# One layer of a hybrid diffusion block: attention scores of both maps on the two halves of the array, exponentials in SBUF, tanh for the gate, one reciprocal root for all heads

## The chip, the cores and the metric

The kernel runs on one core of a Trainium2 chip. The metric is the device time of one execution in microseconds (us); the median of several runs counts.

## What is computed

One mixer layer works on 512 latent tokens and 256 context tokens, 1024 channels wide. One input projection feeds three branches: A, a gated linear recurrence in both directions (LRU); B, differential attention with 8 heads; C, a gated MLP over chunks of 128 positions (SGU). Each is multiplied by a gate path and projected; the three are merged by sigmoid gates, projected once more and normalized. The change touches branch B most:

```python
def diff_attn_core(q, k, v, lam):
    s = jnp.einsum('bqhmd,bkhmd->bhmqk', q.astype(f32), k.astype(f32)) * (DIFF_HEAD_DIM ** -0.5)
    p = jax.nn.softmax(s, axis=-1)
    w = p[:, :, 0] - lam * p[:, :, 1]
    return jnp.einsum('bhqk,bkhe->bqhe', w, v.astype(f32)).astype(v.dtype)

def diff_head_out(o, g, lam_init):
    of = o.astype(f32)
    of = of * lax.rsqrt(jnp.mean(jnp.square(of), axis=-1, keepdims=True) + RMS_EPS)
    of = of * g.astype(f32) * (1.0 - lam_init)

def merge_branches(h_a, g_a, attn, g_b, sgu, g_c, gates, w_branch, w_out):
    y_a = (h_a * jax.nn.silu(g_a)) @ w_branch[0]
    y_b = (attn * jax.nn.silu(g_b)) @ w_branch[1]
    y_c = (sgu * jax.nn.silu(g_c)) @ w_branch[2]
    s_a, s_b, s_c = jnp.split(jax.nn.sigmoid(gates), N_BRANCH, axis=-1)
    return (s_a * y_a + s_b * y_b + s_c * y_c) @ w_out
```

Here m counts the two maps of a head (64 channels each), so a head has 128 channels of q and k.

## The kernel before

All matrix products keep single precision by splitting each operand into a high and a low part (`split`, L53 to L55: ACT casts the high part, DVE subtracts for the low one) and adding three products, high x high, high x low and low x high (`mm3`, L57 to L64). Weights stream from DRAM through three raw buffers on the SP queue (L100, L103); ACT casts the high part (L121), and POOL, or DVE from the LRU stage on, subtracts the low part (L122). Tile pools decide when a buffer comes free. PE runs its matmuls in the order of the program; the other engines are ordered by a list scheduler, with priorities and with the small pieces of work (`chore`, `drain`) placed by their stated costs.

The stages follow each other:
- *Head*: modulation, the projections q, k and kc of heads 0 and 1, and v.
- *Attention loop*, 32 steps (8 heads, 4 blocks of 128 queries). A table (`fill`, L158 to L171) puts the projections of later heads between the steps. A step has the scores of both maps (`scores`, L695 to L708), the softmax (L710 to L723: DVE's maximum `mxn`, ACT's exponential `e` with its sum), the combination of the maps on DVE (L726 to L730), and, a step later, six transposes on PE (L735) and the split of the transposed weights (L746, L748). After a head's fourth block come the product with v (`values`), the mean square `ms` by a matmul with a matrix of ones (L761), Ln and Exp on ACT for the reciprocal root (L762, L763), and a product on POOL (L764). The gate of branch B is a Sigmoid on ACT (L670). These functions lie in different table sets of ACT, so ACT loads a table when it changes between them.
- *LRU stage*, 8 blocks of channels, software pipelined: block i + 1 is projected (`xa`, `xac`, then ACT's copies `pad`, L865 and L867), block i's gates `ri` are computed and pass through sigmoid, tanh and square (`decay`), `merge_gate(i - 1)` and `merge_b(i - 1)` multiply the gate `gt` and the projection `y` of branch B, which reads its operand from `hsB` (the split of `ob`, made ahead of the loop). The results `ha` go to DRAM (`pa_d`, L947) and come back later as `pa` (L1026).
- *SGU and the end*: `sv` (its PSUM tiles freed by `vz`, L1041, which adds a bias row `bvv`), gating, the projections of the other two branches, the output projection and the layer norm.

In the scores before, a head's q of map m stands with its high and low parts on the two halves of the partitions, and k likewise, so that one matmul over 128 rows adds two products:

```python
PE.matmul(sp[:, sl], qds[h][:, 2 * m + j, qs], kds[h][:, m, sl],
          start=(j == 0), stop=(j == 1))
```

For this layout `q_evac` (L527) and `k_split` (L554) work on 64 partitions at a time, and a DMA from POOL's queue copies each half of q to the other half. The exponentials of the second map are written over its scores in PSUM.

Of the kernel before, what the change touches and what calls it, by code (L numbers as in the profile page):

```python
# [10 lines left out]
F32 = mybir.dt.float32  # L11
# [18 lines left out]
def block_kernel(ctx, tc, x, c, cctx_in, c_ctx, w_ada, b_ada, w_in, b_in, conv_w, conv_b,  # L30
# [160 lines left out]
    for i in range(9):  # L191
        if i < 7:
            want("cm", win, (i + 1) * P)
        if i > 1:
            want("cm", win, D + (i - 2) * P)
        if i > 0:
            want("cm", win, 10 * D + (i - 1) * P)
            want("cm", w_branch[0, 1], (i - 1) * P)
# [25 lines left out]
    V.memset(tiny, 2.0 ** -100)  # L224
    sc16 = cp.tile([P, 16], F32, name="sc16")
# [18 lines left out]
    with tc.tile_pool(name="hd", bufs=1) as hd:  # L244
# [186 lines left out]
        S.preload_act_table_set("natural_log_exp_and_others")  # L431
# [4 lines left out]
        V.tensor_scalar(vbias, colC[:, 32:40], lam1, None, op0=ALU.mult)  # L436
        V.tensor_scalar(gcol, colB[:, 104:105], 1.0 - (0.8 - 0.6), None, op0=ALU.mult)
# [30 lines left out]
    at = tc.alloc_tile_pool(name="at", bufs=1, reuse_waits="tile")  # L468
    ropc = at.tile([P, T], F32, name="ropc")
# [3 lines left out]
    vhl, qds, kds, sbs = {}, {}, {}, {}  # L473
# [54 lines left out]
    def q_evac(h, ps):  # L528
        n = f"q{h}"
        z = z_evac(ps, bcol(16 + h), n)  # L530
        rope(z, n)


        def hi():
            qds[h] = at.tile([P, 4, T], F32R, tag="qd", bufs=2, name="qd" + n)
            qd = qds[h]
            for m in range(2):
                a = slice(64 * m, 64 * m + 64)
                if h < 2:
# [10 lines left out]
        chore(0.7, n, hi, 4 * h - 5)  # L550
        chore(0.6, n, lambda: fin(0))
        chore(0.6, n, lambda: fin(1))

    def k_split(n, h, z, sl):  # L554

        def hi():
            if h not in kds:
                kds[h] = at.tile([P, 2, TA], F32R, tag="kd", bufs=2, name=f"kd{h}")
            kd = kds[h]
            for m in range(2):  # L560
                a = slice(64 * m, 64 * m + 64)
                if n[1:] in "01":
                    S.copy(kd[a, m, sl], z[a])
                else:
                    V.tensor_copy(kd[a, m, sl], z[a])  # L565

        def lo(m):
            kd = kds[h]
            a, b = slice(64 * m, 64 * m + 64), slice(64 - 64 * m, 128 - 64 * m)
            V.tensor_tensor(kd[b, m, sl], z[a], f(kd[a, m, sl]), ALU.subtract)  # L570
        w = (sl.stop - sl.start) / 960
        chore(w + 0.15, n, hi, 4 * h - 5)
        chore(w + 0.07, n, lambda: lo(0))
        chore(w + 0.07, n, lambda: lo(1))
# [47 lines left out]
    def units(kind, i):  # L622
# [39 lines left out]
        def u():  # L662
# [7 lines left out]
            S.activation(sg, ps, AF.Sigmoid, bias=bcol(40 + i))  # L670
# [4 lines left out]
            S.preload_act_table_set("natural_log_exp_and_others")  # L675
# [14 lines left out]
    es, sms, wts = {}, {}, {}  # L690
# [4 lines left out]
    def scores(i):  # L695
# [4 lines left out]
        sps = []  # L700
        for m in range(2):
            sp = big_t(f"s{i}_{m}")
            for sl in (slice(0, 512), slice(512, TA)):
                for j in range(2):
                    PE.matmul(sp[:, sl], qds[h][:, 2 * m + j, qs], kds[h][:, m, sl],  # L705
                              start=(j == 0), stop=(j == 1))
            sps.append(sp)
        return sps  # L708

    def softmax(i, sps):  # L710
# [27 lines left out]
    def wt_split(i, tp):  # L738
        h, qt = divmod(i, 4)
        if qt == 0:  # L740
# [6 lines left out]
        with hp(0):  # L747
            V.tensor_tensor(wts[h][1][:, :, qs], src, f(wts[h][0][:, :, qs]), ALU.subtract)  # L748

    def values(h, alloc=acc_t):  # L750
# [3 lines left out]
        sq = at.tile([P, T], F32, tag="sq", bufs=1, name=f"sq{h}")  # L754
# [4 lines left out]
    def rms(h, sq):  # L759
        pm = (acc_t if h < 7 else big_t)(f"ms{h}")[:, 0:T]  # L760
# [65 lines left out]
    dr = ctx.enter_context(tc.tile_pool(name="dr", bufs=1, space=bass.MemoryType.DRAM))
# [452 lines left out]
```

## Time and profile before

| | us |
|---|---|
| median of 3 runs | 1040.11 (1037.9 to 1040.95) |
| the profiled execution | 1038.81 |
| its span | 1037.0 |
| PE busy | 974.0 (94%) |
| DVE busy | 663.6 (64%) |
| ACT busy | 526.1 (51%) |
| POOL busy | 155.7 (15%) |
| chain that ended last: PE, DVE, ACT, DMA | 66%, 16%, 10%, 4% |

A busy share is an average over the whole span. Waits are read place by place: a row of the waits gives the engine and line that waited, what released it, the time in all, how often, and the longest. PE's busy time counts matmuls with modelled ends, so neighbouring matmuls overlap in the records; the pace is read from their starts. The granted clock (PEclk) is a share of TensorE's full clock.

### The profile page before, as it was taken

How to read it: one execution, taken by the hardware profiler on the slowest of the kernel's cores; microseconds unless marked ns; L12 is line 12 of the kernel's file. 1: busy time of each engine (PE TensorE's matmuls, PEld its weight loads, DVE VectorE, ACT ScalarE, POOL GpSimd, SP SyncE). 2: the span in 40 equal slices, each digit the busy share in tenths (PEclk: the TensorE clock that was granted, in tenths of full speed). 3: DMA queues.
4: the chain of work that ended last, by engine and by line, in shares of the span. 5: the costliest groups of instructions: out<-in, count | busy, mean ns of one | idle time of the engine just before them, and what ended most of it. 6: DMA issues, size and time to landing. Idle time of an engine off the chain costs nothing.

```text
span 1037.0 us, 14225 instructions
## 1 busy us (share of the span) xinstructions
PE 974.0 (94%) x5719; PEld 844.0 (81%) x5719; DVE 663.6 (64%) x1024; ACT 526.1 (51%) x741; POOL 155.7 (15%) x117
## 2 busy tenths in 40 slices
PE   5997799989989998999999999599999999999996
PEld 4796688878878886888888888598889988888896
DVE  4479788788788663787777776348433356424567
ACT  3145856647647796897777794213231234332221
POOL 2143424333243252000000000000000000000002
PEclk8999999989989999999999999799999999999998
DMA  9933220130130132113333223534332232654312
GB/s 299 296 103 84 62 61 21 42 101 21 41 102 21 41 102 70 43 51 102 102 102 92 82 92 92 189 107 132 95 99 82 82 102 82 236 171 145 98 61 82
DMA packets 148184, 103.41 MB, mean 100 GB/s; under 512 B 3629, under 2 KB 143382, under 8 KB 148118
## 3 DMA queue, kind: packets, MB, share of 16 engines
q1 hardware_dynamic: 146054, 96.11, 30.4%
q0 software_dynamic: 1920, 6.29, 2.3%
q8 instruction: 45, 0.74, 0.3%
q14 instruction: 21, 0.17, 0.1%
q10 hardware_dynamic: 144, 0.10, 0.0%
HBM read 94.10 MB, written 4.19 MB: 95 GB/s over the span
## 4 chain that ended last, share of the span: by engine, by line
PE 66%; DVE 16%; ACT 10%; DMA 4%; issue 3%; SPq 1%; POOL 0%; POOLq 0%; ACTq 0%; DVEq 0%
PE y L62 4%; PE gt L62 4%; PE gt L64 4%; PE gt L63 4%; PE y L64 4%; PE y L63 4%; DVE mxn L715 2%; DVE e L730 2%; DVE kd L565 2%; PE out L62 1%; PE u L62 1%; PE u L64 1%; PE u L63 1%; PE out L64 1%; PE out L63 1%
## 5 line engine op out<-in xcount | busy, mean ns | idle before, releaser
L121 ACT CAST w<-raw 128x1024 fp32r<-128x1024 f32 x96 | 99.7, 1044 | 83.5 <-PE y L64 20.0
L122 DVE TENSOR_TENSOR w<-raw,w 128x1024 fp32r<-128x1024 f32 x71 | 86.4, 1222 | 66.9 <-ACT w L121 66.9
L62 PE MATMUL gt<-xhl,w 128*128 128x512 f32 x192 | 75.6, 394 | 1.3 <-ACT pad L865 1.3
L63 PE MATMUL gt<-xhl,w 128*128 128x512 f32 x192 | 74.8, 390 | 0.0
L64 PE MATMUL gt<-xhl,w 128*128 128x512 f32 x192 | 74.8, 390 | 0.0
L705 PE MATMUL s<-kd,qdq 128*128 128x512 f32 (+1 forms) x256 | 58.7, 368 | 15.6 <-ACT e L720 6.0
L122 POOL TENSOR_TENSOR w<-raw,w 128x1024 fp32r<-128x1024 f32 x25 | 61.0, 2445 | 67.4 <-ACT w L121 67.4
L705 PEld LDWEIGHTS s<-kd,qdq 128*128 128x128 f32 x256 | 44.5, 196 | 27.1 <-issue 12.7
L715 DVE TENSOR_REDUCE mxn<-s 128x1 f32<-128x768 f32 x64 | 58.3, 949 | 7.5 <-PE s L705 7.5
L720 ACT ACTIVATE e<-s,mxn 128x768 f32<-128x768 f32 x32 | 28.8, 900 | 50.9 <-DVE mxn L715 50.8
L1162 POOL PARTITION_BROADCAST grb<-grs x8 | 3.8, 581 | 322.4 <-DVE grs L1159 322.4
L62 PEld LDWEIGHTS gt<-xhl,w 128*128 128x128 f32 x192 | 36.1, 188 | 9.1 <-ACT pad L865 1.5
L64 PEld LDWEIGHTS gt<-xhl,w 128*128 128x128 f32 x192 | 36.0, 188 | 7.7
L63 PEld LDWEIGHTS gt<-xhl,w 128*128 128x128 f32 x192 | 36.1, 188 | 7.0
L947 POOL DMA_DIRECT2D pa_d<-ha x8 | 4.4, 551 | 227.4 <-DVE ha L946 227.4
L730 DVE SCALAR_TENSOR_TENSOR e<-s,sm,e 128x768 f32<-128x768 f32 x32 | 32.6, 1017 | 6.5 <-ACT e L723 5.7
L54 ACT CAST vh<-v 128x128 fp32r<-128x128 f32 x48 | 12.4, 264 | 42.7 <-PE v L64 19.5
L842 ACT ACT_TABLE_LOAD x25 | 32.1, 1283 | 0.5
L62 PE MATMUL xa<-xhl,w 128*128 128x512 f32 x64 | 26.3, 411 | 4.8 <-ACT pad L865 4.8
L748 DVE TENSOR_TENSOR wtl<-t,wth 128x768 fp32r<-128x768 f32 x32 | 30.3, 950 | 0.6 <-ACT wth L746 0.5
L723 ACT ACTIVATE e<-e,sm 128x768 f32<-128x768 f32 x32 | 29.9, 934 | 0.2 <-DVE sm L722 0.2
L842 ACT ACTIVATE rt<-ri,colB 128x770 f32<-128x770 f32 x32 | 27.7, 906 | 2.5 <-PE ri L64 1.8
(457 smaller groups left out, 3233.0 us busy)
## 6 DMA issues: line engine op xcount, KB each, us to landing
raw<-in_w_in_dram SPq DMA_DIRECT2D x96, 512.0 KB, 3.9
raw<-in_w_branch_dram SPq DMA_DIRECT2D x24, 512.0 KB, 4.0
ada<-in_w_ada_dram SPq DMA_DIRECT2D x6, 1024.0 KB, 9.6
qdq<-qdq POOLq DMA_DIRECT2D x16, 256.0 KB, 3.2
adg<-in_w_ada_dram SPq DMA_DIRECT2D x8, 512.0 KB, 6.6
raw<-in_w_out_dram SPq DMA_DIRECT2D x8, 512.0 KB, 3.4
xtok<-in_x_dram SPq DMA_DIRECT2D x4, 512.0 KB, 5.7
ada<-in_w_ada_dram SPq DMA_DIRECT2D x4, 512.0 KB, 5.9
```

What stands on the lines that cost most here:

```text
L62: PE.matmul(ps, ah, bh, start=(first and i == 0), stop=False)
L63: PE.matmul(ps, ah, bl, start=False, stop=False)
L64: PE.matmul(ps, al, bh, start=False, stop=(last and i == n - 1))
L121: S.copy(h, raws[j])
L122: state["lo"].tensor_tensor(l, raws[j], f(h), ALU.subtract)
L705: PE.matmul(sp[:, sl], qds[h][:, 2 * m + j, qs], kds[h][:, m, sl], start=(j == 0), stop=(j == 1))
L715: V.tensor_reduce(mxn[:, m:m + 1], sps[m][:, 0:TA], mybir.AxisListType.X, ALU.max, negate=True)
L720: S.activation(e, sps[m][:, 0:TA], AF.Exp, bias=mxn[:, m:m + 1], accum_out=sm[:, m:m + 1])
L723: S.mul(es[i][0], es[i][0], sm[:, 0:1])
L730: V.scalar_tensor_tensor(e0, e1, sm[:, 1:2], e0, op0=ALU.mult, op1=ALU.add)
L748: V.tensor_tensor(wts[h][1][:, :, qs], src, f(wts[h][0][:, :, qs]), ALU.subtract)
L842: order[0] = S.activation(out, in_, fn, **kw)
```

## The change

It does the following.
- q and k are kept in their natural layout: high and low parts each over 128 partitions, map 0 on the lower 64, map 1 on the upper 64. The splits take one instruction where they took two, and q's DMAs are dropped. The scores are twelve matmuls over 64 rows, the maps alternating between the two halves of the array (`tile_position`); the product of the low parts is left out, as everywhere else in the kernel.
- Both maps' exponentials go to SBUF.
- The gate's sigmoid is computed as 0.5 tanh(x/2) + 0.5, on ACT by Tanh and Identity.
- The mean square of each head comes from a matmul with 32 columns of ones on one quarter of the array's columns, and is copied into `msb`. Behind the last head one Ln and one Exp take all heads; the result goes through DRAM (`rs_d`) and comes back over all partitions, and DVE multiplies it into `ob` (`hs_b`). This and the split of `ob` stand behind step 0 (heads 0 to 3) and step 1 (heads 4 to 7) of the LRU loop.
- `merge_gate(i)` moves a step ahead, and its weight with it; `xa1` and `xac1` use the larger PSUM tiles; `macc` is allocated in step 1; `xac0` stands ahead of the last head's product.
- The bias row `bvv` is loaded ahead of `pa`, and the last block of `pa` is loaded from POOL's queue.
- Some tiles are allocated ahead of the stage that first uses them.

```diff
+    halfc = cp.tile([P, 1], F32, name="halfc")
+    hb = cp.tile([P, 8], F32, name="hb")
...
-        S.preload_act_table_set("natural_log_exp_and_others")
...
+    wts[0] = tuple(at.tile([P, 6, T], F32R, tag="wt" + n, name=f"wt{n}0") for n in "hl")
...
+    sqs0 = at.tile([P, T], F32, tag="sq", bufs=1, name="sq0")
+    msb = at.tile([P, 2, T], F32, name="msb")
...
-            qds[h] = at.tile([P, 4, T], F32R, tag="qd", bufs=2, name="qd" + n)
+            qds[h] = at.tile([P, 2, T], F32R, tag="qd", bufs=2, name="qd" + n)
...
+                V.tensor_scalar(qds[h][:, 0, :], z, 0.125, None, op0=ALU.mult)
...
+        def lo():
             qd = qds[h]
-            for m in range(2):
...
-            V.scalar_tensor_tensor(qd[a, 2 * m + 1, :], z[a], 0.125, f(qd[a, 2 * m, :]),
+            V.scalar_tensor_tensor(qd[:, 1, :], z, 0.125, f(qd[:, 0, :]),
                                    op0=ALU.mult, op1=ALU.subtract)
-            G.dma_start(qd[b, 2 * m:2 * m + 2, :], qd[a, 2 * m:2 * m + 2, :])
...
+                V.tensor_copy(kds[h][:, 0, sl], z)
...
+        def lo():
             kd = kds[h]
-            for m in range(2):
...
-            V.tensor_tensor(kd[b, m, sl], z[a], f(kd[a, m, sl]), ALU.subtract)
+            V.tensor_tensor(kd[:, 1, sl], z, f(kd[:, 0, sl]), ALU.subtract)
...
-            S.activation(sg, ps, AF.Sigmoid, bias=bcol(40 + i))
+            S.activation(sg, ps, AF.Tanh, bias=hb[:, i:i + 1], scale=0.5)
+            S.activation(sg, sg, AF.Identity, bias=halfc, scale=0.5)
...
-            S.preload_act_table_set("natural_log_exp_and_others")
...
-        for m in range(2):
-            sp = big_t(f"s{i}_{m}")
-            for sl in (slice(0, 512), slice(512, TA)):
-                for j in range(2):
-                    PE.matmul(sp[:, sl], qds[h][:, 2 * m + j, qs], kds[h][:, m, sl],
-                              start=(j == 0), stop=(j == 1))
+        sps = [big_t(f"s{i}_{m}") for m in range(2)]
+        for sl in (slice(0, 512), slice(512, TA)):
+            for j, (jq, jk) in enumerate(((0, 0), (0, 1), (1, 0))):
+                for m in range(2):
+                    a = slice(64 * m, 64 * m + 64)
+                    PE.matmul(sps[m][:, sl], qds[h][a, jq, qs], kds[h][a, jk, sl],
+                              start=(j == 0), stop=(j == 2), tile_position=(64 * m, 0))
...
-            e = sps[1][:, 0:TA]
-            if m == 0:
-                e = at.tile([P, TA], F32, tag="e0", bufs=2, name=f"e0_{i}")
+            e = at.tile([P, TA], F32, tag=f"e{m}", bufs=2 - m, name=f"e{m}_{i}")
...
-        with hp(0):
+        with hp(qt == 3):
             V.tensor_tensor(wts[h][1][:, :, qs], src, f(wts[h][0][:, :, qs]), ALU.subtract)
...
-        PE.matmul(pm, ones, sq, start=True, stop=True)
-        S.activation(sq, pm, AF.Ln, bias=epst)
-        S.activation(sq, sq, AF.Exp, scale=-0.5)
-        G.tensor_tensor(ob[:, h, :], ob[:, h, :], sq, ALU.mult)
+        r = slice(32 * (h % 4), 32 * (h % 4) + 32)
+        PE.matmul(pm[r, 0:T], ones[:, 0:32], sq, start=True, stop=True,
+                  tile_position=(0, 32 * (h % 4)))
+        order[0] = S.copy(msb[r, h // 4, :], pm[r, 0:T])
...
+    rs_d = dr.tile([H, T], F32, name="rs_d")
+    act(msb, msb, AF.Ln, bias=epst)
+    act(msb, msb, AF.Exp, scale=-0.5)
+    for h in range(H):
+        r = 32 * (h % 4)
+        G.dma_start(rs_d[h:h + 1, :], msb[r:r + 1, h // 4, :])
     at.release()
...
+    def hs_b(h):
+
+        if h not in rsb:
+            rsb[h] = lr.tile([P, T], F32, tag="rsb", bufs=1, name=f"rsb{h}")
+        nc.sync.dma_start(rsb[h], rs_d[h].partition_broadcast(P))
+        V.tensor_tensor(ob[:, h, :], ob[:, h, :], rsb[h], ALU.mult)
+        split(hs[:, 0, h, :], hs[:, 1, h, :], ob[:, h, :])
...
-    for h in range(8):
-        split(hs[:, 0, h, :], hs[:, 1, h, :], ob[:, h, :])
...
-            ps = acc_t(f"xa{i + 1}")
+            ps = (acc_t if i else big_t)(f"xa{i + 1}")[:, 0:T]
...
+        if i == 0:
+            merge_gate(0)
         if i < 8:
             gates(i, 0)
-        if i > 0:
-            merge_gate(i - 1)
-        if i < 8:
+            if i > 0:
+                merge_gate(i)
             gates(i, 1)
             decay(i)
         if i < 7:
             lru_w(i + 1)
             conv_split(i + 1)
+        for h in ((0, 1, 2, 3), (4, 5, 6, 7))[i] if i < 2 else ():
+            hs_b(h)
...
+    bvv = bcast(b_in[0, 7 * D:8 * D], "bvv")
     pa = g3.tile([P, KT, T], F32, tag="h2", name="pa")
     hsA = g2.tile([P, 2, KT, T], F32R, tag="hs", name="hsA")
-    for g in range(8):
+    for g in range(7):
         nc.sync.dma_start(pa[:, g, :], pa_d[g])
+    G.dma_start(pa[:, 7, :], pa_d[7])
...
-    proj_tokens(vz, bcast(b_in[0, 7 * D:8 * D], "bvv"), "sv")
+    proj_tokens(vz, bvv, "sv")
```

Three places show how instructions move. First PE, one step of the attention loop; `s_0` and `s_1` are the score tiles of the two maps. Before:

```order
L705 MATMUL s_0_939<-kd_673,qdq_676 128x512 x2
L705 MATMUL s_0_939<-kd_673,qdq_676 128x256 x2
L705 MATMUL s_1_944<-kd_673,qdq_676 128x512 x2
L705 MATMUL s_1_944<-kd_673,qdq_676 128x256 x2
```

Of the change:

```order
L705 MATMUL s_0_930<-kd_684,qdq_686 128x512
L705 MATMUL s_1_931<-kd_684,qdq_686 128x512
L705 MATMUL s_0_930<-kd_684,qdq_686 128x512
L705 MATMUL s_1_931<-kd_684,qdq_686 128x512
L705 MATMUL s_0_930<-kd_684,qdq_686 128x512
L705 MATMUL s_1_931<-kd_684,qdq_686 128x512
L705 MATMUL s_0_930<-kd_684,qdq_686 128x256
L705 MATMUL s_1_931<-kd_684,qdq_686 128x256
```

Two more pairs of 256 columns follow. Eight matmuls, map by map, have become twelve that alternate between the maps.

Second ACT, between the last head of attention and the first gates of the LRU stage; `pad` is the copy that frees the tiles of `xa` and `xac`, `lwh` and `xch` the high parts that the gates read. Before:

```order
L121 CAST w_3844<-raw_3593 128x1024
L762 ACT_TABLE_LOAD
L762 ACTIVATE sq_3732<-ms_3760,epst 128x512
L763 ACT_TABLE_LOAD
L763 ACTIVATE sq_3732<-sq_3732 128x512
L865 ACTIVATE pad<-xa_3683,colC 128x512
L867 ACTIVATE pad<-xac_3735,colC 128x256
L54 CAST hsB<-ob 128x512 x4
L853 CAST lwh_3791<-lw_3781 128x512
L54 CAST hsB<-ob 128x512 x4
L881 CAST xch_3798<-xc_3786 128x770
```

Of the change:

```order
L825 ACT_TABLE_LOAD
L825 ACTIVATE msb<-msb,epst 128x1024
L825 ACT_TABLE_LOAD
L825 ACTIVATE msb<-msb 128x1024
L121 CAST w_3990<-raw_3745 128x1024
L884 ACTIVATE pad<-xa_3769,colC 128x512
L886 ACTIVATE pad<-xac_3799,colC 128x256
L872 CAST lwh_3892<-lw_3882 128x512
L900 CAST xch_3899<-xc_3887 128x770
L884 ACTIVATE pad<-xa_3903,colC 128x512
L886 ACTIVATE pad<-xac_3934,colC 128x256
L54 CAST hsB<-ob 128x512
```

The Ln and Exp have moved ahead of the weight cast and are twice as wide; of the eight casts of hsB one is left here, and the others have moved behind gates and decays of steps 0 and 1.

Third DVE at the end of the LRU stage; `hsA` is the low part of a split of `pa`, `vz` empties an `sv` tile. Before, all eight hsA rows and then four vz rows stood there. Of the change:

```order
L971 TENSOR_TENSOR ha_5601<-ha_5601,sga_5700 128x512
L55 TENSOR_TENSOR hsA<-pa,hsA 128x512
L1071 TENSOR_TENSOR vz<-sv_0_5725,bvv 128x256
L1071 TENSOR_TENSOR vz<-sv_1_5757,bvv 128x256
L55 TENSOR_TENSOR hsA<-pa,hsA 128x512 x6
L1071 TENSOR_TENSOR vz<-sv_2_5787,bvv 128x256
L55 TENSOR_TENSOR hsA<-pa,hsA 128x512
L1071 TENSOR_TENSOR vz<-sv_3_5813,bvv 128x256
```

The first two vz have moved ahead of seven of the eight hsA rows, behind one of them, which is that of the block loaded from POOL's queue.

## Rows read from the trace of the kernel before

**Rows 1.** Stretches of 25 us: PE, PEld, DVE, ACT, POOL busy; PEclk; DMA share; GB/s.
```profile
100.00:125.00 25.00, 22.33 (x114) 18.75 (x114) 17.60 (x34) 24.08 (x35) 7.65 (x4) 0.93 0.15 43
125.00:150.00 25.00, 19.50 (x106) 16.88 (x107) 23.07 (x37) 9.83 (x18) 9.04 (x6) 0.93 0.28 79
200.00:225.00 25.00, 21.15 (x119) 18.84 (x118) 24.34 (x39) 14.29 (x26) 11.48 (x5) 0.86 0.29 85
400.00:425.00 25.00, 20.21 (x97) 16.66 (x96) 12.51 (x19) 12.75 (x19) 3.65 (x3) 0.86 0.22 64
```

**Rows 2.** PE's waits: line, what released it, us in total, times, longest us.
```profile
PE sv L62 <- DVE vz L1041: 11.7, 1, 11.7
PE v L62 <- DVE vl L55: 6.8, 5, 4.7
PE s L705 <- ACT e L720: 6.0, 3, 2.2
PE s L705 <- issue: 5.4, 1, 5.4
PE xa L62 <- ACT pad L865: 4.8, 1, 4.8
PE s L705 <- DVE e L730: 4.3, 4, 1.9
```

**Rows 3.** The chain that ended last, one step's scores: start us, us, engine, line.
```profile
354.75 1.40 PE s L705 x8
```

**Rows 4.** Timeline around 32-column tiles of PE: start us, us, instruction, idle before.
```profile
950.29 0.39 PE L64 MATMUL y<-hsC,w 128*128 128x512 f32 x1
950.61 1.69 PEld L1156 LDWEIGHTS gr<-adg,w32o 128*32 128x32 f32 x64 [0.35 <-issue]
950.61 1.95 PE L1156 MATMUL gr<-adg,w32o 128*32 128x128 f32 x64
...
952.49 0.19 PEld L62 LDWEIGHTS y<-hsC,w 128*128 128x128 f32 x1 [0.20 <-issue]
952.49 0.50 PE L62 MATMUL y<-hsC,w 128*128 128x512 f32 x1
```

**Rows 5.** Timeline of DVE and POOL ahead of the wait called issue.
```profile
123.16 0.67 DVE L524 TENSOR_TENSOR t1k<-t1k,rops 128x512 f32<-128x512 f32 x1
...
123.43 5.36 POOL L122 TENSOR_TENSOR w10l<-raw,w10h 128x1024 fp32r<-128x1024 f32 x2 [1.45 <-issue]
...
123.93 2.67 DVE L525 TENSOR_TENSOR zk<-zk,t1k 128x512 f32<-128x512 f32 x1
...
126.51 2.29 DVE L729 TENSOR_TENSOR sm<-sm,nlam 128x1 f32<-128x1 f32 x1
...
128.93 1.00 DVE L730 SCALAR_TENSOR_TENSOR e<-s,sm,e 128x768 f32<-128x768 f32 x1
```

**Rows 6.** Groups by line and form, ACT: busy us, mean ns, idle before.
```profile
L670 ACT ACT_TABLE_LOAD x8 | 10.3, 1283 | 0.1
```

**Rows 7.** Timeline of DVE and PE at step 16.
```profile
205.32 3.92 DVE L565 CAST kd<-zc 64x256 fp32r<-64x256 f32 x2
...
213.98 0.96 PE L705 MATMUL s<-kd,qdq 128*128 128x512 f32 x4 [1.96 <-ACT e L720]
216.83 1.62 PE L705 MATMUL s<-kd,qdq 128*128 128x512 f32 x4 [1.89 <-DVE e L730]
```

**Rows 8.** Timeline at the start of the LRU stage, ACT and PE.
```profile
417.01 2.17 ACT L54 CAST hsB<-ob 128x512 fp32r<-128x512 f32 x4
...
428.24 3.29 ACT L842 ACTIVATE rt<-ri,colB 128x770 f32<-128x770 f32 x4
...
442.71 0.50 PE L62 MATMUL gt<-xhl,w 128*128 128x512 f32 x1 [1.27 <-ACT pad L865]
```

**Rows 9.** End of the LRU stage: the last write's issue, and DMAs (KB each, median us to landing).
```profile
647.72 0.54 POOL L947 DMA_DIRECT2D pa_d<-ha  x1 [13.23 <-DVE ha L946]
...
pa<-pa_d SPq DMA_DIRECT2D x8, 256.0 KB, 6.0
pa_d<-ha POOLq DMA_DIRECT2D x3, 256.0 KB, 2.6
```

More of the change, by code (lines that the diff above doesn't have):

```diff
@@ L468, in block_kernel @@
     at = tc.alloc_tile_pool(name="at", bufs=1, reuse_waits="tile")
+    vhl, qds, kds, sbs, wts = {}, {}, {}, {}, {}
+    wts[0] = tuple(at.tile([P, 6, T], F32R, tag="wt" + n, name=f"wt{n}0") for n in "hl")
+    for h in range(2):
+        vhl[h] = tuple(at.tile([P, 6, P], F32R, tag="v" + n, bufs=3, name=f"v{n}{h}")
+                       for n in "hl")
+    sqs0 = at.tile([P, T], F32, tag="sq", bufs=1, name="sq0")
+    msb = at.tile([P, 2, T], F32, name="msb")
     ropc = at.tile([P, T], F32, name="ropc")
@@ L688, in block_kernel @@
         drain(2.0)
-    es, sms, wts = {}, {}, {}
+    es, sms, order = {}, {}, [None]
     def hp(on):
@@ L739, in wt_split @@
         h, qt = divmod(i, 4)
-        if qt == 0:
+        if qt == 0 and h > 0:
             wts[h] = (at.tile([P, 6, T], F32R, tag="wth", name=f"wth{h}"),
@@ L753, in values @@
         mm3(ps, vhl[h], wts[h], ix, ix)
-        sq = at.tile([P, T], F32, tag="sq", bufs=1, name=f"sq{h}")
+        sq = at.tile([P, T], F32, tag="sq", bufs=1, name=f"sq{h}") if h > 0 else sqs0
         S.activation(sq, ps, AF.Square, bias=vbias[:, h:h + 1])
@@ L835, in block_kernel @@
     state["lo"] = V
-    order = [None]
-    def act(out, in_, fn, **kw):
-        with tc.issue_after(order[0].ins) if order[0] is not None else ExitStack():
-            order[0] = S.activation(out, in_, fn, **kw)
+    a2s = {(0, 0): lr.tile([P, NJ], F32, tag="a2", bufs=1, name="a200")}
+    has[0] = lr.tile([P, T], F32, tag="ha", bufs=2, name="ha0")
+    sgt = {"sga0": lr.tile([P, T], F32, tag="sga", bufs=1, name="sga0"),
+           "sgm10": lr.tile([P, T], F32, tag="sgm", bufs=2, name="sgm10")}
+    ri0 = {(0, 0, 0): lr.tile([P, NJ], F32, tag="ri0", bufs=3, name="rt000")}
+    rsb = {0: lr.tile([P, T], F32, tag="rsb", bufs=1, name="rsb0")}
+    def hs_b(h):
[4 more added lines that the diff above has]
+        split(hs[:, 0, h, :], hs[:, 1, h, :], ob[:, h, :])
     def lru_dma(g):
@@ L916, in lru_scan @@
     def lru_scan(g):
-        ha = lr.tile([P, T], F32, tag="ha", bufs=2, name=f"ha{g}")
+        ha = has[g] if g == 0 else lr.tile([P, T], F32, tag="ha", bufs=2, name=f"ha{g}")
         for d in range(2):
@@ L982, in block_kernel @@
             conv_in(i + 1, ps, True)
-            ps = acc_t(f"xac{i + 1}")
+            ps = (acc_t if i else big_t)(f"xac{i + 1}")
             proj_cm(ps[:, 0:TC], W, C, 0, TC)
@@ L1021, in silu_gate @@
             ps = None
-    pa = g3.tile([P, KT, T], F32, tag="h2", name="pa")
-    hsA = g2.tile([P, 2, KT, T], F32R, tag="hs", name="hsA")
-    for g in range(8):
-        nc.sync.dma_start(pa[:, g, :], pa_d[g])
     def bcast(src, name):
@@ L1032, in bcast @@
         return t
+    bvv = bcast(b_in[0, 7 * D:8 * D], "bvv")
+    pa = g3.tile([P, KT, T], F32, tag="h2", name="pa")
+    hsA = g2.tile([P, 2, KT, T], F32R, tag="hs", name="hsA")
+    for g in range(7):
+        nc.sync.dma_start(pa[:, g, :], pa_d[g])
+    G.dma_start(pa[:, 7, :], pa_d[7])
     def proj_tokens(dst, bias, name):
```

68 lines of the change are left out of this document (33 added, 35 removed).

## Prediction

> **What bounds the kernel now.** I read five views in this order: the busy table of the page, TensorE's waits, the stretches of 25 us, the chain that ended last, and then the timeline around each long wait. PE (TensorE) is busy for 94% of the span, so a gain must come from shorter PE work, from the few long waits of PE, or from the granted clock after them. [Rows 1] gives the clock as a share of 2.4 GHz, the upper of its two levels; the lower, 1.2 GHz, reads as 0.5. A mean below 1.00 in a stretch means that PE idled and then ran for some time at the lower level. [Rows 2] lists what PE waited for. Leaving out the head of the program, which the change leaves alone, there are three places:
> - the attention loop: the waits for `vl`, ACT's `e`, "issue" and DVE's `e` add to 6.8 + 6.0 + 5.4 + 4.3 = 22.5 us, and the stretches around three of them ran at 0.93, 0.93 and 0.86;
> - the start of the LRU stage: 4.8 us for `pad`, in a stretch at 0.86;
> - the first `sv` matmul behind the LRU stage: 11.7 us.
>
> About 0.3%, 3.1 us, is the least that a measurement of this kernel can tell from no change. The sum is made against the profiled execution, 1038.8 us; the median of the three runs, 1040.1, is 1.3 above it, inside their spread of 3 us.
>
> **Scores.** Before, a step's eight matmuls take 1.40 us where nothing disturbs them [rows 3]. They stream 4 x 512 + 4 x 256 = 3072 columns, so a column costs 0.456 ns. After, there are twelve matmuls of 64 rows, alternating between the upper and the lower half of the array. If each pair runs side by side, 2304 column times are left: 1.05 us. If each weight load stands in line instead, the loads set the pace: 64 loads of 32 columns took 1.69 us [rows 4], 0.026 each, so one of 128 columns takes 0.106 and twelve take 1.27. I take 1.2, nearer the loads, because a load must come before each pair and the loads of one half repeat.
> Then the change of tiling. In [rows 4] PE goes from whole-array matmuls to 32-column tiles and back. The first tile starts 0.32 us after the last `y`, where such matmuls follow each other at 512 x 0.456 = 0.23: 0.09 lost. On the way back the weight loader idles 0.20, and the first `y` takes 0.50 against 0.39: 0.31 lost. That is 0.40 for one excursion. No row shows 64-row tiles, so 0 and 0.40 are my two ends; I take 0.40, the only excursion of the trace. A step is then 1.6 against 1.40: 32 x 0.2 = **+6**. Bounds: 1.05 without the 0.40 gives -11, 1.27 with it +9.
> The page TensorEngine Tiling (Array Packing) of the Trainium skill says under Key Properties that different tiles load and multiply in parallel, but that changing the tiling mode drains the engine. This rule speaks against a 1 us burst between whole-array matmuls; by its first half alone the term would be -6 (1.2 us a step), by both it stays +6, and [rows 4] agrees with the drain.
>
> **Mean squares.** Each of the eight `ms` matmuls is now a 32-column tile too, among whole-array ones: 8 x 0.40 = **+3** (bounds 0 and +3).
>
> **The waits of the attention loop.** They have four causes that the change touches. (a) The second map's exponentials stay in the `s` tile in PSUM until DVE has combined both maps, so scores two steps on wait for that DVE instruction. After, the tile is free as soon as ACT has written e1 to SBUF. The wait called "issue" is such a one: POOL's two subtractions ran for 5.36 us and beside them a 128x512 add took 2.67 and a 128x1 product 2.29 [rows 5], so the combine at 128.93 came late. It goes: 5.4, less 1.2 because the `mxn` reduction of the next step comes late as well, plus the clock of that stretch (0.07 x 25 = 1.75): **-6**. (b) 29 of the 61 table loads go, at 1283 ns of ACT each ([rows 6], one group of eight; L762, L763 and L720 have like ones). In the attention loop they come ahead of the exponentials for which the scores wait. (c) A head's k splits ran as four casts and four subtractions on 64 partitions, two casts of which took 3.92 us together ahead of the reductions; they become two and two on 128 partitions of the same row length. Steps 16 and 24 each lost about 3.5 to both (1.96 and 1.89 at step 16 [rows 7]), with some 1.5 of clock: I take **-4** each; and the third wait for ACT's `e`, 2.2 with its clock (1.75 in the stretch 100 to 125), **-4**. (d) The wait of 4.7 for `vl` loses the table loads and half the splits ahead of it: **-3**. What stays late: the short waits of some 0.5, and DVE, which is busy for 24.3 of 25 us at step 16 [rows 1]. Sum **-21**; bounds -10, if DVE's queue instead of the dropped steps holds the reductions, and -29.5, all idle time and the 7 us that the three stretches lost to the clock.
> The 16 DMAs of the q splits leave POOL's queue. Nothing waited long for them; I cost this at 0, since the lo halves are written in place and cover nothing else.
>
> **Start of the LRU stage.** Before, PE lost 4.8 and 1.3 (`gt`, behind `pad` [rows 8]), and 25 x 0.14 = 3.5 to the clock [rows 1]: 9.6. The 4.8 goes: `pad` no longer stands behind Ln and Exp with their loads for head 7 alone. But ACT's queue there gains one Ln and one Exp over 128x1024, each behind a load, and they now stand ahead of the weight cast and of both `pad` groups. I count about 1.8 before `gt0`, and 2.5 before the first `ri`, which waits for `xch`; 1.0 for the next `xch`. In step 1, `merge_gate(1)` (`gt1`) waits for xa2's `pad`, which stands behind step 0's decay (eight instructions of about 0.82 as in [rows 8], and a load), a weight cast, and three hsB casts of 0.54 [rows 8]: some 4.6 past the matmuls that cover it. `merge_b(0)` needs hsB 6 and 7, which stand behind step 1's decay: a load 1.28, four exponentials or tanhs and two squares at 0.82, the casts of `lwh` and `xch`, two hsB casts of 0.54, a DVE subtraction, 9.5 in all, against 18 matmuls x 0.23 = 4.1 of `y0` that are ready: about 6. The new losses are 1.8 + 2.5 + 1.0 + 4.6 + 6 = 15.9. **+6**; bounds 0 (ACT reaches hsB early, while PE works at gates) and +10 (the clock falls again). The eight DMAs to DRAM and back (2.6 and 6.0 us for 256 KB [rows 9]) lie beside step 0 and cost 0; without that cover they would add their 8 us once.
>
> **The `sv` wait.** `vz` waited for the bias row, which was queued on SP behind eight `pa` loads that themselves wait for the last write of `pa_d`. Now the bias row goes ahead of them. But DVE's program has the subtraction of hsA for one `pa` block ahead of `vz`, and that block is the one loaded last, from POOL's queue. Write at 647.7, 2.6 to land, a load of 6.0 [rows 9], then 0.6 of cast, 0.7 of subtraction, 0.4 of `vz`: 658 in place of 661.1. With the bias off the shared DMA engines I take **-4**; bounds -2 and -8.
>
> The merge-gate matmuls only move. Sum: 6 + 3 - 21 + 6 - 4 = -10, so **1029 us**.
>
> **Rivals.**
> 1. *The two halves take turns* (slower). Then the twelve matmuls take 4608 columns, 2.10 us, and a step 2.5: +35 in place of +6, **1058**. It decides from 1.91 us a step, where the 10 us are used up. For it: no row here has two row tiles at once, and each map's three products gather in one PSUM tile. Against it: in [rows 4] 64 matmuls of 128 columns took 1.95 us, though at 0.456 ns a column one after the other they need 3.7; column tiles do overlap. This is also the case in which the change does not do what it says. The page TensorE: Matmul & The Clock Gate, Part 3, of the Trainium skill tells of four row tiles at 3.07 times the pace of one, in place of 4; an estimate by that, 1.05 x 4 / 3.07 = 1.37, would add 5 to the sum. No run here shows it yet.
> 2. *POOL holds DVE's combine* (no change). The combine now reads both operands from SBUF. In [rows 5] a 128x512 operation on SBUF took 0.67 just ahead of POOL's subtractions and the next one 2.67 beside them, while the combine with e1 in PSUM took 1.00. With each overlap 2 us later, the transposes wait and half of the 21 stays: **1039**. For it: POOL runs 11.5 us of 25 at step 16 [rows 1]. Against: transposes come a step later than the combine.
> 3. *The LRU start costs nothing new and the `sv` wait nearly goes*, 6 and 8 us better: **1015**. For it: ACT is idle about half of the stretch from 400 to 425 [rows 1]. Against: the order of ACT's queue, above.
>
> **How the numbers follow.** Forecast 0.60, spread 1019 to 1037; rival 1 0.15, rival 2 0.12, rival 3 0.13. Rival 1 alone lies above 1044, and 1012 is rival 3 with a few us of its bounds: the range is 1012 to 1044. Faster: 0.58 of the forecast, 0.13, and 0.02 of rival 2, 0.73. Same: 0.02 and 0.07, 0.09. Slower: 0.15 and 0.03, 0.18.
>
> **What would show it.** Right: a step's scores at 1.5 to 1.7 us with pairs starting within 0.05 us of each other; no PE wait over 2 us between 95 and 395 us; `gt` and `y` waits of several us at the start of the LRU stage; an `sv` wait of 7 to 9. Wrong: scores above 1.9, combines of 2 us or more with transposes waiting for them, or no new wait behind hsB and `pad`.

## The result and the profile after

The change makes the kernel slower: 1062.2 us (1061.1 to 1063.1, 4 runs) against 1039.3, a ratio of 1.0227 with a 95% interval of 1.0215 to 1.0239. The forecast was 1029 us, range 1012 to 1044.

The waits of PE in the kernel after (line, what released it, us in all, times, longest), to be set beside [rows 2]:

```profile
PE o L63 <- DVE wtl L745: 16.1, 6, 3.0
PE sv L62 <- DVE vz L1071: 10.6, 1, 10.6
PE gt L62 <- ACT pad L884: 5.7, 2, 3.8
PE y L62 <- ACT hsB L54: 5.1, 1, 5.1
...
PE gb L62 <- DVE n8sp L461: 4.0, 1, 4.0
PE ri L62 <- ACT xch L900: 3.4, 1, 3.4
PE v L62 <- DVE vl L55: 3.2, 2, 2.4
...
PE s L705 <- ACT e L717: 1.4, 2, 1.0
```

The scores, which waited 15.6 us for ACT, DVE and "issue", now wait 1.4. In their place `o`, the product of the attention weights with v, which waited 0.2 us in all before, waits 16.1 us, in six of the eight heads. What happens there is seen in ACT and DVE, then POOL, then PE around one of them (timeline of the kernel after, start us, us; idle before in brackets):

```profile
177.57 0.81 ACT L743 CAST wth<-t 128x768 fp32r<-128x768 f32 x1
177.91 0.69 DVE L535 TENSOR_TENSOR t1q<-t1q,rops 128x512 f32<-128x512 f32 x1
179.79 2.84 DVE L536 TENSOR_TENSOR zq<-zq,t1q 128x512 f32<-128x512 f32 x1 [1.19 <-POOL zq L533]
182.56 0.94 DVE L745 TENSOR_TENSOR wtl<-t,wth 128x768 fp32r<-128x768 f32 x1
183.43 1.81 DVE L714 TENSOR_REDUCE mxn<-s 128x1 f32<-128x768 f32 x2
```
```profile
177.96 1.80 POOL L533 TENSOR_TENSOR zq<-zq,ropc 128x512 f32<-128x512 f32 x1 [6.54 <-DVE t1q L532]
179.72 2.37 POOL L122 TENSOR_TENSOR w<-raw,w 128x1024 fp32r<-128x1024 f32 x1
```
```profile
180.46 0.39 PE L62 MATMUL o<-wth,vh 128*128 128x512 f32 x1
183.56 0.69 PE L63 MATMUL o<-wtl,vh 128*128 128x512 f32 x1 [2.71 <-DVE wtl L745]
184.05 0.63 PE L64 MATMUL o<-wth,vl 128*128 128x512 f32 x1
...
188.69 0.40 PE L63 MATMUL o<-wtl,vh 128*128 128x512 f32 x1
```

`wth` is cast by 178.4, so `wtl` could start. But DVE's program has the last addition of q's rotation ahead of it (L536, `chore` in `rope`). That addition waits 1.19 us for POOL's product and then takes 2.84 beside POOL's weight subtraction. PE idles for 2.71, and the matmuls behind the wait follow each other at 0.43 us, then at 0.23: eight of them at the lower clock level (the granted clock of the stretch from 175 to 200 is 0.93). Five of the six waits have such matmuls behind them; the first, of 2.07 us, has not. In the program before, `wtl` and both `mxn` stood ahead of the addition (DVE, then POOL, before):

```profile
177.01 1.81 DVE L715 TENSOR_REDUCE mxn<-s 128x1 f32<-128x768 f32 x2
178.74 0.95 DVE L748 TENSOR_TENSOR wtl<-t,wth 128x768 fp32r<-128x768 f32 x1
...
179.67 1.48 DVE L525 TENSOR_TENSOR zq<-zq,t1q 128x512 f32<-128x512 f32 x1
```
```profile
178.20 2.40 POOL L122 TENSOR_TENSOR w<-raw,w 128x1024 fp32r<-128x1024 f32 x1
```

The rows show why the place matters so much. The addition ends 0.55 us after POOL's subtraction in both programs (181.15 behind 180.60 before, 182.63 behind 182.09 after), so the earlier it starts, the longer it keeps DVE.

The second place is the start of the LRU stage (ACT, and PE with its waits):

```profile
424.71 1.06 ACT L825 ACTIVATE msb<-msb 128x1024 f32<-128x1024 f32 x1
428.94 1.04 ACT L121 CAST w<-raw 128x1024 fp32r<-128x1024 f32 x1 [3.16 <-issue]
430.00 0.69 ACT L884 ACTIVATE pad<-xa,colC 128x512 f32<-128x512 f32 x1
...
436.66 0.62 ACT L872 CAST lwh<-lw 128x512 fp32r<-128x512 f32 x1 [5.60 <-DMA lw<-in_lru_wx_dram]
438.97 0.83 ACT L900 CAST xch<-xc 128x770 fp32r<-128x770 f32 x1 [1.69 <-DVE xc L893]
```
```profile
425.00:450.00 25.00, 19.54 (x88) 16.02 (x87) 14.54 (x20) 12.57 (x17) 4.20 (x8) 0.86 0.31 86
450.00:475.00 25.00, 21.05 (x101) 17.54 (x101) 22.21 (x28) 22.81 (x29) 0.00 (x0) 0.93 0.27 85
475.00:500.00 25.00, 19.49 (x84) 15.62 (x84) 19.15 (x23) 14.00 (x19) 0.00 (x0) 0.86 0.25 73
```

The weight cast (428.94) starts when the last matmul of `xac1` has ended (428.85) and so, by all signs, waits for the place of its weights, and the `pad` copies, whose inputs stood ready at 411 and 414, wait behind it. The stretches below (columns as in [rows 1]) run at 0.86, 0.93 and 0.86.

Milestones of PE, each the first matmul of its kind, give the account. `xa0`, the end of attention, starts at 405.8 after against 395.8 before: +10.0. `ga0`, when two steps of the LRU loop are done, starts at 494.3 against 464.2; one merge gate more lies ahead of it after, 24 matmuls or 5.5 us: +24.6, so that the LRU start costs 14.6. The end of the `sv` wait stands 23.9 later (685.0 against 661.1) and the end of the span 23.3: about 0.7 came back by the end of that wait, which is itself 1.0 shorter (10.6 against 11.7), and 0.6 behind it.

### The profile page after: what moved, and what is told of

Same layout as the page of the kernel before. It is cut to its first block, busy times and chain, and to the rows that moved or that the text cites. A ratio compares the mean times of both kernels' runs of the same rounds, so it can differ in the third digit from the quotient of the medians.

```text
span 1060.3 us, 14381 instructions
## 1 busy us (share of the span) xinstructions
PE 985.6 (93%) x5847; PEld 840.1 (79%) x5847; DVE 656.5 (62%) x992; ACT 488.1 (46%) x708; POOL 139.2 (13%) x102
## 4 chain that ended last, share of the span: by engine, by line
PE 54%; issue 28%; DVE 7%; POOL 4%; DMA 3%; ACT 3%; SPq 1%; POOLq 0%; DVEq 0%; ACTq 0%
PE y L62 3%; PE gt L62 3%; PE gt L64 3%; PE y L64 3%; PE gt L63 3%; PE y L63 3%; DMA ada<-in_w_ada_dram 2%; DVE zq L536 2%; PE s L705 2%; PE out L62 1%; PE u L62 1%; PE u L64 1%; PE u L63 1%; PE out L64 1%; PE out L63 1%
## 5 line engine op out<-in xcount | busy, mean ns | idle before, releaser
L717 ACT ACTIVATE e<-s,mxn 128x768 f32<-128x768 f32 x64 | 57.6, 902 | 80.6 <-DVE mxn L714 80.6
L705 PEld LDWEIGHTS s<-kd,qdq 64*128 64x128 f32 x384 | 32.4, 186 | 16.7 <-issue 8.8
L705 PE MATMUL s<-kd,qdq 64*128 64x256 f32 (+1 forms) x384 | 43.7, 355 | 1.4 <-ACT e L717 1.4
L727 DVE SCALAR_TENSOR_TENSOR e<-e,sm,e 128x768 f32<-128x768 f32 x32 | 32.6, 1019 | 10.8 <-ACT e L720 9.6
L63 PE MATMUL o<-wtl,vh 128*128 128x512 f32 x48 | 22.6, 471 | 16.1 <-DVE wtl L745 16.1
L62 PE MATMUL gb<-xhl,w 128*128 128x512 f32 x64 | 26.4, 413 | 5.6 <-DVE n8sp L461 4.0
L62 PE MATMUL y<-hsB,w 128*128 128x512 f32 x64 | 25.6, 400 | 5.1 <-ACT hsB L54 5.1
```

What stands on the lines that cost most here:

```text
L62: PE.matmul(ps, ah, bh, start=(first and i == 0), stop=False)
L63: PE.matmul(ps, ah, bl, start=False, stop=False)
L705: PE.matmul(sps[m][:, sl], qds[h][a, jq, qs], kds[h][a, jk, sl], start=(j == 0), stop=(j == 2), tile_position=(64 * m, 0))
L717: S.activation(e, sps[m][:, 0:TA], AF.Exp, bias=mxn[:, m:m + 1], accum_out=sm[:, m:m + 1])
L727: V.scalar_tensor_tensor(e0, e1, sm[:, 1:2], e0, op0=ALU.mult, op1=ALU.add)
```

## Experiments

**e1: DVE's order alone.** The rule is an ordering between two instructions of DVE.

```diff
-        chore(0.6, name, lambda: V.tensor_tensor(z, z, t[0], ALU.add),
+        def add():
+            with tc.issue_after(last[0].ins) if last[0] is not None else ExitStack():
+                V.tensor_tensor(z, z, t[0], ALU.add)
+        chore(0.6, name, add,
...
-            V.tensor_tensor(wts[h][1][:, :, qs], src, f(wts[h][0][:, :, qs]), ALU.subtract)
+            last[0] = V.tensor_tensor(wts[h][1][:, :, qs], src, f(wts[h][0][:, :, qs]),
+                                      ALU.subtract)
```

> The kernel after the change, with one rule more for DVE: the last addition of the rotation of q or k stands behind the subtraction for the low part of the transposed weights (wtl), as it did before. Nothing is added or left out. Theory A (in six heads the product with v waits for wtl, which stands behind that addition, which waits for POOL; each wait of 2.1 to 2.9 us is followed by some 17 matmuls at the lower clock): the six waits, 16.1 us, and the clock behind them, some 8, go: 1062 - 24 = 1038, between 1034 and 1042. Theory B (DVE is late as a whole, and the order only decides who waits): the waits turn up at the scores or transposes instead, and the time stays above 1050.

Measured: 1038.4 us, 23.8 less than the change, 1.0003 of before (0.9987 to 1.0019). Theory A's number holds; of its reasons the 17 slow matmuls behind each wait do not, since some eight came behind five of the six. The `o` waits are gone, and those of `v` for `vl` rose from 3.2 to 6.1 us. The same DVE instructions, and POOL's subtraction, now run so (timeline):

```profile
172.73 0.95 DVE L749 TENSOR_TENSOR wtl<-t,wth 128x768 fp32r<-128x768 f32 x1
173.60 1.81 DVE L718 TENSOR_REDUCE mxn<-s 128x1 f32<-128x768 f32 x2
175.33 1.55 DVE L539 TENSOR_TENSOR zq<-zq,t1q 128x512 f32<-128x512 f32 x1
```
```profile
173.94 2.40 POOL L122 TENSOR_TENSOR w<-raw,w 128x1024 fp32r<-128x1024 f32 x1
```

`xa0` starts at 381.4: attention is now 14.4 us shorter than before the change, and the LRU stage takes nearly all of it back (`ga0` at 468.5 against 464.2, with the one merge gate of 5.5 us more ahead of it).

**e2: the same waits, covered on PE.** All 18 products remain.

```diff
-        mm3(ps, vhl[h], wts[h], ix, ix)
+        for kt in range(6):
+            PE.matmul(ps, vh[:, kt, :], wh[:, kt, :], start=(kt == 0), stop=False)
+            PE.matmul(ps, vl[:, kt, :], wh[:, kt, :], start=False, stop=False)
+        for kt in range(6):
+            PE.matmul(ps, vh[:, kt, :], wl[:, kt, :], start=False, stop=(kt == 5))
```

> The kernel after the change, with DVE's order left as it is; only the 18 matmuls of the product with v are put in another order, the six that read wtl at the end, so that 12 matmuls x 0.23 = 2.8 us of work lie ahead of the first that needs it. Theory A: waits of 2.1 to 2.9 us are covered all but some 0.5 in total, and PE does not drop its clock: 1038 to 1041. Theory B: DVE still delivers the maxima late, so the next scores or transposes wait instead: above 1050.

Measured: 1069.2 us, 7 more than the change. Theory A's number is a miss, theory B's holds, though `v` and not the scores or transposes wait. The waits of `o` fell to 1.6 us in all, but PE reached the next block of v sooner and waited there, 21.7 us for what DVE does behind the addition; the `sv` wait grew too, from 10.6 to 13.4 (waits of PE):

```profile
PE v L62 <- DVE vl L55: 12.0, 4, 3.3
PE v L62 <- DVE ob L759: 9.7, 3, 3.3
...
PE o L756 <- DVE wtl L745: 1.6, 5, 0.5
```

So it is not the one operand `wtl` that is late: an addition that sits some 4 us on DVE, waiting and stretched, delays the whole chain behind it (`wtl`, `mxn`, the combination, `vl`), and PE meets it at the next point. In e1 the addition starts later, takes 1.55 for 2.84, and runs while ACT computes the exponentials that DVE's next instruction waits for. This is theory B's form of the same cause; e1 shows that the order sets it.

**e3 and e11: the scores part alone.** The kernel before with the diff's `q_evac`, `k_split` and `scores`; e11 adds e1's rule.

> The kernel before the change, with one part of it alone: q and k in the natural layout, their splits over 128 partitions, no DMAs of q, and the scores as twelve matmuls with both maps side by side. Exponentials, gate, mean squares, LRU stage and end are those of before. Theory A: the scores themselves take 1.25 us a step in place of 1.40 and are not what makes the change slow, but DVE's order with the addition ahead of wtl comes with this part, so the product with v waits in six heads here too: 1039 + 24 - 3 for the scores, less some of the old waits of the scores, that is 1050 to 1060. Theory C (the order comes with the exponentials in SBUF, the tanh or the mean squares at the end): no such waits, 1030 to 1038. Theory D (the prediction's rival: the two halves take turns): a step's scores above 1.9 us, and 1065 or more.

> The kernel of e3 (before, with the scores part alone) and e1's rule, so that the addition stands behind wtl: this prices the scores part without the order that came with it. Theory A: the 10.2 us of waits for wtl go, with some 4 of clock: 1047 - 14 = 1033, between 1030 and 1037, so the scores part by itself is worth 2 to 9 us. Theory J (the prediction's sum: the change of tiling costs more than the shorter scores give back): 1043 or above.

Measured: e3 1046.9 us, 1.0086 of before (1.0058 to 1.0114); e11 1030.0, 0.992 (0.990 to 0.994). The order comes with the scores part: in e3 `o` waits for `wtl` in six heads, in e11 not at all. The row of e3's waits:

```profile
PE o L63 <- DVE wtl L735: 10.2, 6, 2.0
```

e3 lies below its range since these waits are shorter than after the change (2.0 at most, not 3.0) and none of them has slow matmuls behind it: the granted clock is 1.00 in the stretches around them. A step's scores take 1.25 us in both where they wait for nothing, so the rival of turns and theory J fall. Freed of its order, the part is worth 8.6 us. Why the scheduler lists the addition first with the scores part is open: no run tests it.

**e7 and e8: two other parts undone,** on top of e1: the second map's exponentials back in PSUM (e7), and the gate as one Sigmoid (e8).

```diff
-            e = at.tile([P, TA], F32, tag=f"e{m}", bufs=2 - m, name=f"e{m}_{i}")
+            e = sps[1][:, 0:TA]
+            if m == 0:
+                e = at.tile([P, TA], F32, tag="e0", bufs=2, name=f"e0_{i}")
```
```diff
-            S.activation(sg, ps, AF.Tanh, bias=hb[:, i:i + 1], scale=0.5)
-            S.activation(sg, sg, AF.Identity, bias=halfc, scale=0.5)
+            S.activation(sg, ps, AF.Sigmoid, bias=bcol(40 + i))
```

> The kernel of e1 with one part of the change undone: the second map's exponentials are written over its scores in PSUM again, so that the scores two steps later wait for the combination on DVE. Theory A (the prediction's point (a)): waits of the scores for DVE's e come back, about the 5.4 us beside POOL's subtractions and some short ones, with the clock behind them: +6 to +10, 1044 to 1048. Theory H (with shorter scores and splits the combination is early enough): within 2 us of 1038.

> The kernel of e1 with one part of the change undone: the gate of branch B by Sigmoid again, with the table loads that it brings (15 more in all). Theory A (the prediction's point (b): the loads stood ahead of the exponentials for which the scores wait): waits for ACT's e come back, +4 to +8, 1042 to 1046. Theory I (without Ln and Exp for each head the gate's loads alone find ACT idle): within 2 us of 1038.

Measured: e7 1044.1 us, 5.7 more than e1, near the lower end of theory A (1.0047 of before, 1.0033 to 1.0060, against e1's 1.0003). The scores wait for the combination again, in one place above all:

```profile
PE s L709 <- DVE e L733: 9.3, 6, 6.0
```

e8 is 1038.0, no different from e1: theory I. Its scores wait for ACT's `e` for 1.4 us, as in e1. The 15 loads that it brings back hold no scores. e11 says the same of the rest: it has all 61 loads of the kernel before, and its scores wait nowhere for ACT's `e`.

**e4, e5, e9, e10: the start of the LRU stage.** e4 (on the change) puts the weight cast behind the first `pad` copies. e5 (on e1, with e4's rule) moves `merge_b` a step back. e9 and e10 raise the `pad` copies of block 3, and of block 2 too.

```diff
         if i == 0:
+            state["aft"] = state["pad0"]
             merge_gate(0)
+            state["aft"] = None
...
-        S.copy(h, raws[j])
+        with tc.issue_after(state["aft"].ins) if state.get("aft") else ExitStack():
+            S.copy(h, raws[j])
```
```diff
-        if i > 0:
-            merge_b(i - 1)
+        if i > 1:
+            merge_b(i - 2)
     branch_a(7)
+    merge_b(7)
```
```diff
-            pump()
-            conv_in(i + 1, ps, True)
+            with hp(i in (1, 2)):
+                pump()
+            with hp(i in (1, 2)):
+                conv_in(i + 1, ps, True)
```

(e9 has `(2,)`; `conv_in` of the context block is raised likewise.)

> The kernel after the change, with one rule more for ACT at the start of the LRU stage: the cast of the weight for the block behind the first merge gate stands behind the two pad copies of block 0, and not ahead of them. Theory A (that cast waits for the matmuls of xac1, and the pad copies, whose inputs were there 15 us earlier, wait behind it; the first merge gate, the convolution and the first gates follow late): the waits of 1.9 and 3.4 us and the lower clock behind them go, -7, 1055, between 1052 and 1058; the later waits for pad (3.8) and hsB (5.1) stay. Theory E (the weights of the recurrence, loaded late, hold the first gates anyway): within 2 us of 1062.

> The kernel of e1 (addition behind wtl) with two rules more at the start of the LRU stage: the weight cast of e4 stands behind the pad copies of block 0, and merge_b of a block stands one step later, with its weight, so that hsB 6 and 7 have a whole step more (a third buffer for the merge gates' sigmoids takes the place of the buffer of the broadcast roots). Theory A (the stage loses 14.5 us of waits for pad, xch and hsB and nearly 9 us to the clock behind them, because the late casts stand in ACT's queue ahead of what PE needs): all of these but the wait of gt1 (2.4 to 3.8) go, 1038 - 12 - 4 = 1022, between 1018 and 1027. Theory F (ACT and DVE have more work in steps 0 and 1 than PE, so a later merge only moves the wait to the next pads or gates): above 1030.

> The kernel of e5 with the pad copies of block 3, and the weight cast ahead of them, raised in ACT's order: they stand inside the decay of block 1 and not behind it, its hsB casts and its square roots. Theory A (what still costs in steps 1 and 2 is the place of the pad copies in ACT's queue, not ACT's work): the wait of ga for pad, 8.8 us in e5, goes, with most of the clock behind it (0.80 in the stretch 450 to 475): 1023 - 9 - 3 = 1011, between 1008 and 1016. Theory F (ACT has more to do than PE covers): the wait moves on to the gates of block 2, above 1018.

> As e9, with the pad copies of block 2 and the weight cast of step 1 raised as well. Theory A: the wait of gt1 (3.8 us in e5) goes too, with some clock: 1007, between 1004 and 1011. Theory F: the cast of a weight that waits for its slot now stands ahead of others, and xa3 or gt1 waits for weights instead: 1011 or above.

Measured: e4 1056.9 us, 5.3 less than the change: the first two waits went, but that of `y` for hsB grew from 5.1 to 8.3. e5 1022.7, e9 1012.4, e10 1011.4, which is 0.974 of before (0.972 to 0.975). The numbers of e4, e5 and e9 lie in theory A's ranges, but in e5 not by its sum alone; e10 lies just above its own, at the edge of theory F's. The waits for `xch` and hsB went, a new one of 8.8 us came (theory F's, of `ga` for the next `pad`), and the `sv` wait fell from 12.0 to 2.0: `merge_b(7)` now stands ahead of it and fills 5.4 us of it, and from the last `ga` to the end of that wait it took 18.9 us in place of 23.7. PE's waits in e5, and then in e10:

```profile
PE ga L62 <- ACT pad L890: 8.8, 1, 8.8
...
PE gt L62 <- ACT pad L890: 3.8, 1, 3.8
...
PE sv L62 <- DVE vz L1081: 2.0, 1, 2.0
```
```profile
PE sv L62 <- DVE vz L1084: 2.6, 1, 2.6
...
PE ga L62 <- ACT pad L890: 1.7, 1, 1.7
```

e9 takes the 8.8 down to 1.4 by the place of two copies and a weight cast in ACT's queue alone, so ACT's amount of work was not the bound. e10 removes the 3.8 of `gt` and gains only 1 us, hardly clear of the noise: small waits came in its place, 1.5 us of `ri` for ACT's `rt` among them, and `sv` waits 2.6 for 1.7. It is the best version: 51 us below the change, 27 below the kernel before.

**e6 and e12: the bias row.** On e1; e6 puts the hsA subtractions behind the second `vz`, e12 queues the bias row behind `pa` again.

```diff
-        split(hsA[:, 0, g, :], hsA[:, 1, g, :], pa[:, g, :])
+        S.copy(hsA[:, 0, g, :], pa[:, g, :])
+        with tc.issue_after(state["vz", "sv"].ins):
+            V.tensor_tensor(hsA[:, 1, g, :], pa[:, g, :], f(hsA[:, 0, g, :]), ALU.subtract)
```
```diff
-    bvv = bcast(b_in[0, 7 * D:8 * D], "bvv")
     pa = g3.tile([P, KT, T], F32, tag="h2", name="pa")
...
     G.dma_start(pa[:, 7, :], pa_d[7])
+    bvv = bcast(b_in[0, 7 * D:8 * D], "bvv")
```

> The kernel of e1 with DVE's subtractions for hsA behind the second vz, so that the vz that empty the first two sv tiles wait for the bias row alone. Theory A (the bias row was asked for 6 us ahead of the pa loads, and only the subtraction for the block of pa that POOL loads kept vz back): the sv wait falls from 12.0 to some 5 us, -7, 1031, between 1028 and 1034. Theory G (the bias row, 512 KB, shares the DMA engines with the last write of pa_d, so that it lands no earlier than the pa loads): within 3 us of 1038.

> The kernel of e1 with the bias row queued behind the pa loads again, as before the change. Theory A (the bias row, asked for ahead of them, slows the last write of pa_d, which took 5.7 us to land after the change and 2.6 before, so that what the earlier bias row gives, the later pa loads take back): the write lands in some 2.6 us, the sv wait is 11 to 13 us, and the time stays within 3 us of 1038. Theory K (the early bias row is worth what the prediction said): 4 us slower or more.

Measured: e6 1034.5 us, 3.9 less than e1, between the two theories: the first `sv` wait fell to 5.4, but a second of 2.0 came. e12 1041.4, 2.9 more than e1, between its two theories as well; as shares of before, 1.0025 (1.0013 to 1.0037) and 1.0003 (0.9987 to 1.0019), the two overlap, so it is likely but not shown that the early row is worth 2 to 3 us. Theory A's reason is a miss: the `sv` wait is 14.3, and the load behind the write never starts after 2.6. POOL's `pa` load waits for it for 5.68 us after the change and, with the bias row behind (e12), still for 4.87:

```profile
679.43 0.55 POOL L1060 DMA_DIRECT2D pa<-pa_d  x1 [5.68 <-DMA pa_d<-ha]
```
```profile
652.27 0.55 POOL L1064 DMA_DIRECT2D pa<-pa_d  x1 [4.87 <-DMA pa_d<-ha]
```

In e1 it is 6.28, so between these two profiles the early row costs the write 1.4 us. In the kernel before, where the bias row stood behind too, the last `pa` load started 6.2 us after the write was issued (647.72, [rows 9]), as after the change (673.21 to 679.43):

```profile
653.88 0.32 SPq L1026 DMA_DIRECT2D pa<-pa_d  x1
```

## Why the prediction was wrong

**The step that failed** is the term of -21 for the attention loop: it counted the waits that go and put new ones at nothing. What stands behind an instruction that POOL holds on DVE was asked under rival 2, but of the combination alone and not through the whole queue. The trace after the change shows the addition ahead of `wtl` in all six heads that wait, and [rows 5] had shown an addition of this kind taking 2.67 us beside POOL. Together they make `wtl` about 3 us late in each of six heads, and `o` directly behind the block of v has no cover for it. The runs put this at 23.8 us (e1 against the change). 16.1 of it is idle time; most of the rest fits the lower clock, which cost some 1.7 us behind each of five waits, an estimate from the starts of the matmuls. The sign "no PE wait over 2 us between 95 and 395 us" failed by these waits. Rival 2 itself did not come: the combination took 1.02 us, as before.

**What was right in that term.** The mechanisms (a) and (c): the old waits of the scores fell from 15.6 to 1.4 us, e7 prices (a) at 5.7 (forecast 6), and e11 shows the scores part with its splits at 8.6. With the order restored, attention is 14.4 us shorter, where the terms for scores, mean squares and waits together gave 12. That the two are near is in part luck: scores and mean squares cost less than forecast, and the waits gave less. Point (b), the table loads, held no scores (e8, e11). Point (d) did not come either: the wait for `vl` fell from 4.7 to 2.4, but `gb` waits 1.4 and 4.0 us close behind it, the second while two DVE operations on 16 columns take 2.29 us each beside POOL, and 0.17 otherwise.

**Scores (+6 forecast) and mean squares (+3).** Together they cost some 2 us, an estimate from the rows that follow. The excursion (whole array to tiles and back) was right: in the rows below the scores start 0.21 us after the last v, where such matmuls follow at 0.12, so 0.09 in; 1.25 us lie between the first scores and the next matmul, and that one takes 0.50 for 0.39.

```profile
168.41 0.28 PE L64 MATMUL v<-w10h,xhl 128*128 128x256 f32 x1
168.62 1.31 PE L705 MATMUL s<-kd,qdq 64*128 64x512 f32 x12
169.87 0.50 PE L62 MATMUL q<-xhl,w 128*128 128x512 f32 x1
```

That is 1.45 with both ends. Narrower windows of the same timeline show the six pairs starting at 168.62, 168.96, 169.20, 169.43, 169.54 and 169.66: behind the first they follow at the pace of one map alone, so the pairs do run side by side, and the weight loads are covered, which I had not granted them (1.2). Behind transposes a step of the old kind took 1.48 to 1.67 where nothing waited, not 1.40, and one of the new kind 1.54 counted the same way, so there a step gains nothing and loses nothing. An `ms` with the scores behind it took 2.25 us before (151.06 to 153.31) and 2.23 after, with 0.09 more ahead of it and 0.11 more on the matmul behind.

**Start of the LRU stage (+6 forecast, 14.6 measured).** The five waits were named at their places: 1.8, 2.5, 1.0, 4.6 and 6 were expected, 1.89, 3.37, about 0.2, 3.76 and 5.09 came. What the sum left out is the clock behind them: the three stretches at 0.86, 0.93 and 0.86 lose up to 25 x 0.35 = 8.75 us (some of the lower clock may lie inside the waits). Waits of 14.3 and this, less the old 9.6, make 13.5 of the 14.6. The clock stood in the range only ("the clock falls again"), while the old clock loss was counted as a gain. e4, e5 and e9 show that the waits come from places in ACT's queue, as the prediction had it.

**The `sv` wait (-4 forecast, -1.0 measured).** The place was right, the size was not: the load that waits for the last write of `pa_d` could start not 2.6 but 6.2 us after the write was issued. The 2.6 was the median of three writes; the last `pa` load of the kernel before, 6.2 us behind its write, was the row to read.

## What to carry to other kernels

When a change alters how long one engine's block seems to take, read the new program order of the other engines instruction by instruction, and for each instruction that waits for a third engine ask what stands behind it: here one addition ahead of a subtraction cost more than the whole change gave. Covering such a wait on the engine that idles only moved it here (e2); moving the waiting instruction to where its own engine would wait anyway removed it (e1). And give each new wait its clock: behind five of the six `o` waits (2.7 to 2.9 us) PE ran some eight matmuls at the lower level, which cost about half as much again as the waits; behind the sixth (2.07) and behind e3's (1.6 to 2.0) it did not.

## What was not expected of the hardware

Two matmuls of 64 rows on the two halves of the array stream at once at full pace: in the burst at 168.62 the pairs behind the first follow at 0.23 us for 512 columns and 0.11 to 0.12 for 256, as whole-array matmuls do, so none of their weight loads shows. The change of tiling into and out of that burst costs 0.40 us: 0.09 ahead of the first pair, 0.11 behind it, 0.09 at the end and 0.11 on the first whole-array matmul. The sum is the same as for the 32-column tiles of [rows 4].

The last addition of a rotation (128x512) takes 0.68 us on DVE where POOL is idle, as it is beside k's at 164.95 after the change. Beside POOL's 128x1024 subtraction q's ended 0.5 to 0.6 us after that subtraction, whether it had started with it (2.84) or 1.4 to 1.5 us later (1.48 before, 1.55 in e1), in six heads of each of the three kernels. In e1 `wtl` beside POOL's product and `mxn` beside its subtraction, which both read a PSUM tile, kept their usual 0.95 each.

A 256 KB write to DRAM took 2.4 to 2.6 us to land as a median, but as the last of its kind, with other loads on the queues, it held the load that waits for it for 4.9 to 6.5 us (e12, the change, e1, e6). In e5, where the bias row was asked for 3.9 us ahead of that write and not 0.4, the first `pa` load started 3.6 us after the write was issued.
